# Background modulation of a two-layer diffusion backbone: a third of the dot products as GpSimd product and ScalarE sum, or all of them on VectorE

## The chip, the core and the metric

The kernel runs on one core of a Trainium2 chip. The metric is device time in microseconds for one launch; a change is judged by the median of several runs of the kernel before and of the kernel after. Engines are called by the names that the profile uses: PE (matmul), DVE (VectorE), ACT (ScalarE), POOL (GpSimd), SP (the queue that issues the loads).

## The reference, cut to what matters

The model has two layers. Each is a half-step feed-forward stage, a token mixer and a second feed-forward stage, and each of these takes shift, scale and gate vectors that come from the conditioning. These vectors are what this case is about:

```
for l in range(DEPTH):
    m_lat = (silu(c)     @ mod_w[l] + mod_b[l])   # 9 vectors of 1024 for the 512 latent tokens
    m_ctx = (silu(c_ctx) @ mod_w[l] + mod_b[l])   # the same weights, for the 256 context tokens
    h_lat = ffn_sublayer(h_lat, m_lat, 0, ...)    # rmsnorm, modulate, SwiGLU, gate
    h_ctx = ffn_sublayer(h_ctx, m_ctx, 0, ...)
    ...                                           # mixer, second feed-forward
```

`mod_w[l]` has 1024 x 9216 elements. The kernel holds it transposed as 72 tiles of 128 x 1024 for each layer, so that one entry of the result is the dot product of a tile's row with a vector of 1024. A context vector is not needed for the last four ninths of layer 1.

## The kernel before, in words

**Feed-forward.** Weights come as units of 128 x 1024 float32 (`raw`, by `w_fetch`). Each is split into a high part on ACT (`whi`, L760) and a low part on DVE (`wlo`, L770), and each product runs as three matmuls (L869 to L871). The inner width of 2816 is cut into chunks of 6, 5, 5 and 6 rows. A row is a gate unit and an up unit, each of 8 x 3 matmuls of 512 columns and as many of 256, 96 matmuls for the row in all. Its end is the eviction: ACT takes silu of the gate (L1064), DVE multiplies by the up bank (L1067), ACT rounds to `gh` (L918) and DVE subtracts to `gl` (L921). When the rows of a chunk are done, `w2` multiplies them with the second weight matrix, one output row m after the other; the first m goes through the earlier rows of the chunk first and comes last to the last row, whose `gh` and `gl` it needs then. From the second chunk on, DVE adds its result to `y` (L1108).

**Background.** Of the 144 modulation tiles, 16 are worked in the start (`start`, not touched here), and 128 in the background of the first feed-forward stage by `mods_task`, sixteen tasks of 8 tiles. A task is a generator: `pump` gives it credit, 0.65 for each us of matmul time that the program has written out, and each `yield` takes some back. So background work is written into the engines' queues at points fixed by the program's order and not by the clock of the chip; each engine then goes through its own queue in order. A background dot product (`mod_dot`, L651) therefore stands in DVE's queue among the `wlo`, the evictions and the adds.

A tile of weights (`mw`) has three slots. `mw_get` takes the next one that is loaded; `mw_put` puts the tile on a list, and after the delay that it names `mw_free` closes the tiles up to it and has SP load as many new ones (`mw_load`, L626). SP also issues the loads of `raw` (L749), in order.

Before the change, a tile with t divisible by 3 has its last dot product (the context's, or the latent one where there is no context) worked in two steps: POOL multiplies the tile in place by the vector (L667), and ACT copies it in place with a running sum (L668), written when the tile is freed. The 96 tiles with a context hold 32 such products, the 32 tiles without one hold 10.

At the end of a task, DVE adds the bias to the results (L680).

Of the kernel before, what the change touches and what calls it, by code (L numbers as in the profile page):

```python
# [12 lines left out]
AF = mybir.ActivationFunctionType  # L13
ALU = mybir.AluOpType
# [11 lines left out]
LAT, CTX = 0, 1  # L26
# [42 lines left out]
class Graph:  # L69
# [4 lines left out]
    LAT = 0.15  # L74
# [337 lines left out]
class Model:  # L412
# [241 lines left out]
    def mods_task(self, l, i, groups=(LAT, CTX)):  # L654

        nc = self.nc

        def gen():
            for t in range(i * 8, i * 8 + 8):
                w = self.mw_get()  # L660
                v = groups[-1]
                pool = t % 3 == 0
                if v == CTX or not pool:
                    self.mod_dot(w, l, t, LAT)
                    yield 1.14
                if pool:
                    nc.gpsimd.tensor_tensor(w, w, self.cb[v], op=ALU.mult)  # L667
                    self.mw_put(4.5, lambda w=w, t=t, v=v: nc.scalar.activation(w, w, AF.Copy,  # L668
                                                                                accum_out=self.modc[l][:, v, t:t + 1]))
                else:  # L670
                    if v == CTX:
                        self.mod_dot(w, l, t, v)
                    self.mw_put(1.5, lambda: None)
                yield 0.6
            yield 3.0
            self.mw_free(3)
            s = slice(i * 8, i * 8 + 8)
            bias = self.vec(f"mod_b{l}")[:, s]
            for v in groups:
                nc.vector.tensor_tensor(self.modc[l][:, v, s], self.modc[l][:, v, s], bias, op=ALU.add)  # L680
            self.bg_done.add((l, i))
            yield 0.2
        return ((l, i), gen())
# [2207 lines left out]
```

## Time and profile before

| | |
|---|---|
| median of 3 runs | 3002.24 us (2994.0 to 3002.37) |
| profiled execution, its own time | 3001.87 us |
| its span, first to last instruction | 2999.9 us |
| mean granted clock of PE | 0.966 |

The profile counts an engine as busy while an instruction of the program is on it, a stretched one too. Of the granted clock 1.00 is 2.4 GHz and 0.50 is 1.2 GHz. A row of a timeline gives start and duration in us, and in brackets the idle time ahead of it with what ended that. Matmul records overlap, since they are pipelined, so the distance between starts says more than the duration. A group's line ends with busy time and mean ns of one, then the idle time ahead of the group and what ended most of it.

### The profile page before, as it was taken

The page shows a single profiled execution, that of the slowest core. Times are in us where ns is not written, and L with a number is a line of the kernel's source. Part 1 is how long each engine was busy: PE and PEld are TensorE (multiplying, and loading weights), DVE is VectorE, ACT ScalarE, POOL GpSimd, SP SyncE. Part 2 cuts the span into 40 slices and gives each one's busy share as a digit, 9 for nine tenths or more (in the row PEclk, how much of TensorE's full clock was granted, in tenths as well). Part 3 has the DMA queues.
Part 4 walks back from the last instruction along what each step waited for, and adds up shares of the span by engine and source line. Part 5 has one row for each costly group of instructions (what it writes and reads, how often), then busy time and mean ns, then how long its engine had stood idle before and what let it go on. Part 6 is the DMA issues. An engine that isn't in the chain of part 4 may idle for free. (4 is left out here: it accounts for less than half of the span.)

```text
span 2999.9 us, 42053 instructions
## 1 busy us (share of the span) xinstructions
PE 2838.6 (95%) x16008; PEld 2456.4 (82%) x16008; DVE 1852.1 (62%) x3201; ACT 1084.4 (36%) x1897; POOL 898.4 (30%) x1281
## 2 busy tenths in 40 slices
PE   4999899989999989999999899999998899999997
PEld 3888778877778778888888788888887897888886
DVE  8799989675588667544544753543637694543334
ACT  3433223344477653222213432212224443432222
POOL 4122222352355350243344543343345000300001
PEclk7999999999799999999999899999999999999998
DMA  6365656633000223323233332232333563233332
GB/s 247 105 212 183 203 180 215 239 104 131 6 24 22 82 88 97 100 75 98 71 102 100 96 113 88 79 95 81 91 94 104 183 204 105 92 106 97 97 103 70
DMA packets 140808, 343.55 MB, mean 115 GB/s; under 512 B 13632, under 2 KB 61248, under 8 KB 138560
## 3 DMA queue, kind: packets, MB, share of 16 engines
q1 hardware_dynamic: 140608, 340.88, 35.2%
q8 instruction: 126, 2.06, 0.3%
q14 instruction: 74, 0.61, 0.1%
HBM read 311.53 MB, written 29.29 MB: 114 GB/s over the span
## 5 line engine op out<-in xcount | busy, mean ns | idle before, releaser
L869 PE MATMUL mm<-ahi,whi 128*128 128x512 f32 (+1 forms) x2128 | 740.0, 348 | 20.9 <-ACT ahi L555 16.7
L870 PE MATMUL mm<-alo,whi 128*128 128x512 f32 (+1 forms) x2128 | 735.7, 346 | 10.7 <-DVE alo L556 7.1
L871 PE MATMUL mm<-ahi,wlo 128*128 128x512 f32 (+1 forms) x2128 | 728.5, 342 | 4.6 <-DVE wlo L770 4.6
L770 DVE TENSOR_TENSOR wlo<-raw,whi 128x1024 fp32r<-128x1024 f32 (+2 forms) x391 | 461.4, 1182 | 376.0 <-ACT whi L760 360.4
L760 ACT ACTIVATE whi<-raw 128x1024 fp32r<-128x1024 f32 (+2 forms) x411 | 392.8, 956 | 296.8 <-PE mm L870 161.7
L869 PEld LDWEIGHTS mm<-ahi,whi 128*128 128x128 f32 x2128 | 406.7, 191 | 80.2 <-ACT ahi L555 18.8
L870 PEld LDWEIGHTS mm<-alo,whi 128*128 128x128 f32 x2128 | 406.7, 191 | 61.9 <-DVE alo L556 9.7
L871 PEld LDWEIGHTS mm<-ahi,wlo 128*128 128x128 f32 x2128 | 405.5, 191 | 55.6 <-DVE wlo L770 5.5
L869 PE MATMUL mm<-gh,whi 128*128 128x512 f32 x992 | 350.8, 354 | 13.5 <-ACT gh L918 13.5
L870 PE MATMUL mm<-gl,whi 128*128 128x512 f32 x992 | 349.8, 353 | 1.2 <-DVE gl L921 1.2
L871 PE MATMUL mm<-gh,wlo 128*128 128x512 f32 x992 | 346.8, 350 | 1.4 <-DVE wlo L770 1.4
L651 DVE SCALAR_TENSOR_TENSOR mj<-mw,cb 128x1024 bf16<-128x1024 f32 x182 | 262.6, 1443 | 24.5 <-DMA mw<-in_mod_wT_dram 21.8
L918 ACT ACTIVATE gh<-tmp 128x512 fp32r<-128x512 f32 (+1 forms) x135 | 73.7, 546 | 491.8 <-DVE tmp L1067 490.7
L667 POOL TENSOR_TENSOR mw<-mw,cb 128x1024 f32<-128x1024 f32 x42 | 116.3, 2770 | 379.2 <-DVE mj L651 320.9
L869 PEld LDWEIGHTS mm<-gh,whi 128*128 128x128 f32 x992 | 188.4, 190 | 43.3 <-ACT gh L918 14.9
L2171 POOL TENSOR_TENSOR s5t<-s5pw,s5bb 128x256 f32<-128x256 f32 x128 | 87.0, 708 | 440.4 <-PE mm L2182 353.5
L871 PEld LDWEIGHTS mm<-gh,wlo 128*128 128x128 f32 x992 | 187.8, 189 | 27.9 <-DVE wlo L770 1.9
L870 PEld LDWEIGHTS mm<-gl,whi 128*128 128x128 f32 x992 | 188.3, 190 | 27.1 <-DVE gl L921 2.8
L907 POOL TENSOR_TENSOR S<-S,tmp 128x512 f32<-128x512 f32 (+1 forms) x25 | 27.3, 1094 | 596.7 <-ACT tmp L906 596.2
L1067 DVE TENSOR_TENSOR tmp<-tmp,mm 128x512 f32<-128x512 f32 (+1 forms) x135 | 77.5, 574 | 186.3 <-PE mm L871 186.3
L279 POOL TENSOR_TENSOR S<-S,tmp 128x256 f32<-128x256 f32 (+3 forms) x116 | 134.5, 1162 | 135.4 <-ACT tmp L276 128.7
L1064 ACT ACTIVATE tmp<-mm 128x512 f32<-128x512 f32 (+1 forms) x135 | 63.0, 506 | 274.1 <-PE mm L871 274.1
(463 smaller groups left out, 5188.8 us busy)
## 6 DMA issues: line engine op xcount, KB each, us to landing
raw<-in_w_dram SPq DMA_DIRECT2D x210, 512.0 KB, 3.7
mw<-in_mod_wT_dram SPq DMA_DIRECT2D x128, 512.0 KB, 4.3
raw<-in_w_dram SPq DMA_DIRECT2D x88, 384.0 KB, 3.1
raw<-in_w_dram SPq DMA_DIRECT2D x64, 320.0 KB, 3.0
raw<-in_w_in_dram SPq DMA_DIRECT2D x23, 512.0 KB, 3.5
m0d<-in_mod_wT_dram SPq DMA_DIRECT2D x16, 512.0 KB, 8.0
raw<-in_w_out_dram SPq DMA_DIRECT2D x16, 512.0 KB, 3.3
s5v<-s5v SPq DMA_DIRECT2D x64, 128.0 KB, 3.0
```

Source lines behind the costliest of these rows:

```text
L279: add = lambda e: lambda: e.tensor_tensor(S(), S(), q["t"][:, :n], op=ALU.add)
L651: self.nc.vector.scalar_tensor_tensor(junk, w, 1.0, self.cb[v], op0=ALU.mult, op1=ALU.mult, accum_out=self.modc[l][:, v, t:t + 1])
L667: nc.gpsimd.tensor_tensor(w, w, self.cb[v], op=ALU.mult)
L760: self.nc.scalar.activation(hi[:, :n], raw[:, :n], AF.Copy)
L770: (eng or self.nc.vector).tensor_tensor(lo[:, :n], raw[:, :n], hi[:, :n].bitcast(F32), op=ALU.subtract)
L869: mm(out, whi, xhi, start=first, stop=False)
L870: mm(out, whi, xlo, start=False, stop=False)
L871: mm(out, wlo, xhi, start=False, stop=last)
L918: nc.scalar.activation(hi, src, AF.Copy)
L1064: nc.scalar.activation(st["s", jj, q][:, :n], bk[g][:, cs], AF.Silu)
L1067: nc.vector.tensor_tensor(t[:, :n], t[:, :n], bk[g][:, cs], op=ALU.mult)
L2171: g_.tensor_tensor(o, x, y, op=ALU.mult)
```

## The change

`mods_task` no longer tells tiles apart. For each group (latent, and context where there is one) it runs `mod_dot` on DVE. The product on POOL and the sum on ACT are gone from this task. Every tile is put on the list to be freed with a delay of 1.5 (before: 4.5 where POOL had the product). The credit of a tile with both groups stays 1.14 and 0.6. For a tile with the latent group alone it is 1.14; before, it was 1.14 and 0.6, or 0.6 alone where POOL had it.

```
-                v = groups[-1]
-                pool = t % 3 == 0
-                if v == CTX or not pool:
-                    self.mod_dot(w, l, t, LAT)
-                    yield 1.14
-                if pool:
-                    nc.gpsimd.tensor_tensor(w, w, self.cb[v], op=ALU.mult)
-                    self.mw_put(4.5, lambda w=w, t=t, v=v: nc.scalar.activation(w, w, AF.Copy,
-                                                                                accum_out=self.modc[l][:, v, t:t + 1]))
-                else:
-                    if v == CTX:
-                        self.mod_dot(w, l, t, v)
-                    self.mw_put(1.5, lambda: None)
-                yield 0.6
+                for v in groups:
+                    self.mod_dot(w, l, t, v)
+                    if v != groups[-1]:
+                        yield 1.14
+                self.mw_put(1.5, lambda: None)
+                yield 0.6 if len(groups) > 1 else 1.14
```

## Rows read from the trace of the kernel before

**Rows 1.** The page, busy time of each engine, its share of the span and its instructions.

```profile
PE 2838.6 (95%) x16008; PEld 2456.4 (82%) x16008; DVE 1852.1 (62%) x3201; ACT 1084.4 (36%) x1897; POOL 898.4 (30%) x1281
```

**Rows 2.** The waits of PE from 137 to 600 us: who waited for what, us in total, times, longest.

```profile
PE mm L869 <- ACT gh L918: 13.5, 3, 7.0
PE mm L871 <- DVE wlo L770: 1.4, 1, 1.4
```

**Rows 3.** The timeline of PE, at the first rows of a chunk's first unit (218.03) and around the ends of three chunks: the first matmul on `gh` after each chunk's last row, and the first that needs that last row.

```profile
218.03 0.40 PE L869 MATMUL mm<-ahi,whi 128*128 128x512 f32 x1
...
302.02 0.40 PE L869 MATMUL mm<-gh,whi 128*128 128x512 f32 x1
...
313.42 0.80 PE L869 MATMUL mm<-gh,whi 128*128 128x512 f32 x1 [7.04 <-ACT gh L918]
...
438.98 0.40 PE L869 MATMUL mm<-gh,whi 128*128 128x512 f32 x1
...
451.31 0.79 PE L869 MATMUL mm<-gh,whi 128*128 128x512 f32 x1 [6.27 <-ACT gh L918]
...
580.67 0.39 PE L869 MATMUL mm<-gh,whi 128*128 128x512 f32 x1
...
584.45 0.51 PE L869 MATMUL mm<-gh,whi 128*128 128x512 f32 x1 [0.22 <-ACT gh L918]
```

**Rows 4.** Windows behind the two long waits of PE: stretch and its length, then busy us and instructions of PE, PEld, DVE, ACT and POOL, then the granted clock, the share of the DMA engines and GB/s.

```profile
313.40:319.70 6.30, 5.31 (x14) 3.96 (x15) 5.57 (x11) 2.71 (x5) 1.19 (x1) 0.50 0.33 109
319.70:325.00 5.30, 5.30 (x31) 4.58 (x31) 4.40 (x8) 0.74 (x1) 0.00 (x0) 1.00 0.77 264
...
451.30:456.20 4.90, 4.89 (x13) 3.64 (x14) 4.38 (x8) 2.71 (x5) 0.00 (x0) 0.50 0.42 140
```

**Rows 5.** The timeline of DVE: the evictions L1067 of rows of a chunk, two dot products one behind the other, an undisturbed `gl`, the add that PE released, and the dot product ahead of the eviction at 449.92.

```profile
239.02 0.68 DVE L1067 TENSOR_TENSOR tmp<-tmp,mm 128x512 f32<-128x512 f32 x1
...
294.71 0.69 DVE L921 TENSOR_TENSOR gl<-tmp,gh 128x512 fp32r<-128x512 f32 x1 [0.70 <-ACT gh L918]
...
296.56 1.22 DVE L651 SCALAR_TENSOR_TENSOR mj<-mw,cb 128x1024 bf16<-128x1024 f32 x1
...
297.82 1.22 DVE L651 SCALAR_TENSOR_TENSOR mj<-mw,cb 128x1024 bf16<-128x1024 f32 x1
...
312.03 0.68 DVE L1067 TENSOR_TENSOR tmp<-tmp,mm 128x512 f32<-128x512 f32 x1
...
323.68 1.02 DVE L1108 TENSOR_TENSOR y<-mm,y 128x512 f32<-128x512 f32 x2 [0.90 <-PE mm L871]
...
446.75 3.24 DVE L651 SCALAR_TENSOR_TENSOR mj<-mw,cb 128x1024 bf16<-128x1024 f32 x1
...
449.92 0.68 DVE L1067 TENSOR_TENSOR tmp<-tmp,mm 128x512 f32<-128x512 f32 x1
```

**Rows 6.** The timeline of POOL from 445 to 448 us.

```profile
445.59 3.32 POOL L667 TENSOR_TENSOR mw<-mw,cb 128x1024 f32<-128x1024 f32 x1 [9.52 <-DVE mj L651]
```

**Rows 7.** The instructions of one line of the code, duration in ns as least, median and most, with the first and last start: the dot product (whole run), `wlo` (140 to 590 us), the bias add (137 to 600 us), the product on POOL and the sum on ACT.

```profile
L651 DVE SCALAR_TENSOR_TENSOR mj<-mw,cb x182: 1208/1224/3433, 138.1 to 593.9; 128x1024 bf16<-128x1024 f32 x182
...
L770 DVE TENSOR_TENSOR wlo<-raw,whi x61: 812/1216/3419, 140.5 to 586.2; 128x1024 fp32r<-128x1024 f32 x34, 128x640 fp32r<-128x640 f32 x16, 128x768 fp32r<-128x768 f32 x11
...
L680 DVE TENSOR_TENSOR modc<-modc,vecs x27: 150/160/2372, 165.9 to 574.5; 128x8 f32<-128x8 f32 x27
...
L667 POOL TENSOR_TENSOR mw<-mw,cb x42: 2347/2408/3444, 145.5 to 587.1; 128x1024 f32<-128x1024 f32 x42
...
L668 ACT ACTIVATE mw<-mw x42: 1039/1060/1066, 148.0 to 593.9; 128x1024 f32<-128x1024 f32 x42
```

**Rows 8.** Groups of DVE by line and shape, 170 to 239 us (the second chunk up to the eviction at 239.02; POOL starts six products in it).

```profile
L651 DVE SCALAR_TENSOR_TENSOR mj<-mw,cb 128x1024 bf16<-128x1024 f32 x32 | 45.7, 1430 | 2.7 <-DMA mw<-in_mod_wT_dram 2.1
...
L770 DVE TENSOR_TENSOR wlo<-raw,whi 128x1024 fp32r<-128x1024 f32 x4 | 7.1, 1770 | 0.0
L680 DVE TENSOR_TENSOR modc<-modc,vecs 128x8 f32<-128x8 f32 x4 | 2.8, 712 | 1.9 <-ACT mw L668 1.9
```

**Rows 9.** The same view, 239 to 312 us (up to the eviction at 312.03; POOL starts six products in it).

```profile
L651 DVE SCALAR_TENSOR_TENSOR mj<-mw,cb 128x1024 bf16<-128x1024 f32 x33 | 48.1, 1456 | 2.8 <-DMA mw<-in_mod_wT_dram 2.3
...
L921 DVE TENSOR_TENSOR gl<-tmp,gh 128x512 fp32r<-128x512 f32 x4 | 5.3, 1324 | 2.8 <-ACT gh L918 2.8
```

**Rows 10.** The same view, 323.6 to 449.9 us (from the add that PE released to the eviction at 449.92; POOL starts eleven products in it).

```profile
L651 DVE SCALAR_TENSOR_TENSOR mj<-mw,cb 128x1024 bf16<-128x1024 f32 x54 | 79.0, 1463 | 3.2 <-DMA mw<-in_mod_wT_dram 2.3
L770 DVE TENSOR_TENSOR wlo<-raw,whi 128x1024 fp32r<-128x1024 f32 x10 | 14.4, 1440 | 1.6 <-ACT whi L760 1.6
L921 DVE TENSOR_TENSOR gl<-tmp,gh 128x512 fp32r<-128x512 f32 x4 | 4.9, 1236 | 2.8 <-ACT gh L918 2.8
...
L680 DVE TENSOR_TENSOR modc<-modc,vecs 128x8 f32<-128x8 f32 x8 | 3.2, 437 | 1.2 <-ACT mw L668 1.2
```

**Rows 11.** The waits of DVE from 137 to 600 us.

```profile
DVE mj L651 <- DMA mw<-in_mod_wT_dram: 21.8, 23, 3.6
```

**Rows 12.** Groups of DVE by line and shape, 505 to 600 us, where the tiles have no context group.

```profile
L651 DVE SCALAR_TENSOR_TENSOR mj<-mw,cb 128x1024 bf16<-128x1024 f32 x22 | 32.6, 1481 | 14.9 <-DMA mw<-in_mod_wT_dram 14.9
```

**Rows 13.** DMA issues from 505 to 600 us: the loads of `mw` tiles, their number, size and median us from issue to landing.

```profile
mw<-in_mod_wT_dram SPq DMA_DIRECT2D x30, 512.0 KB, 4.6
```

**Rows 14.** A window over the last chunk's rows, columns as in Rows 4.

```profile
492.00:581.00 89.00, 89.00 (x482) 76.87 (x481) 66.23 (x86) 31.91 (x51) 28.58 (x11) 1.00 0.71 246
```

## The prediction, as it was put on record

> **What bounds the kernel now.** I read the page first: PE is busy for 95% of the span [rows 1], so an edit to work on other engines can only give or take PE's waits, and the clock that is lost behind them. The background runs from the first dot product at 138 us to the last at 594 us [rows 7], so I read PE's waits in that stretch: 13.5 us for `gh` and 1.4 us for `wlo` [rows 2]. The timeline of PE places them [rows 3]: 7.04 us up to 313.42 and 6.27 us up to 451.31, both in the first `w2` unit after a chunk's rows, at the matmul that needs the chunk's last row. The third chunk end, at 580.67, has two hiccups, the first of 0.22 us [rows 3].
>
> Behind each of the two waits the granted clock is 0.50 for a while. From 313.4 PE issues 14 matmuls in 6.3 us, where it issues 31 in 5.3 us at 1.00 [rows 4]; 14 are worth 2.4 us, so 3.9 us are lost. From 451.3 it issues 13 in 4.9 us, worth 2.2 us, so 2.7 us are lost. The first chunk end therefore costs 7.0 + 3.9 = 10.9 us, the second 1.4 + 6.3 + 2.7 = 10.4 us. Together **21.3 us** is all that this stage has to give.
>
> Why is `gh` late? It waits for the eviction L1067 on DVE, and DVE is behind. PE leaves the last row of the chunk at 302.02 [rows 3] and DVE starts its eviction at 312.03 [rows 5]: a lag of 10.0 us, of which the first 3.0 cost nothing (10.0 less the wait of 7.0). At the second end the lag is 449.92 - 438.98 = 10.9 us, of which 10.9 - 7.7 = 3.2 are free; at the third it is about 2.4 us, with some 2 free. DVE's queue is thus the bound wherever its lag at a chunk end exceeds 3 us, and the change is to be costed as DVE time ahead of these three evictions.
>
> **The change part by part.**
>
> *Added on DVE:* 42 dot products, one for each product on POOL [rows 7]. One takes 297.82 - 296.56 = 1.26 us from start to start with its readout [rows 5], 53 us in all.
>
> *Removed from POOL:* 42 products of 2.41 us median [rows 7]. POOL itself holds nothing up, but DVE stands still beside it. The product of 445.59 lasts until 448.9 [rows 6]; the dot product that starts on DVE at 446.75 takes 3.24 us [rows 5] where the median is 1.22 [rows 7]: 2.0 us in which DVE does nothing, just ahead of the eviction at 449.92. I size this by groups against undisturbed durations (dot product 1.224, `wlo` 1.216, bias add 0.160 [rows 7], `gl` 0.69 [rows 5]). From 239 to 312 us: 33 x (1.456 - 1.224) = 7.7 for the dots and 4 x (1.324 - 0.69) = 2.5 for `gl` [rows 9], 10.2 us for six products. From 323.6 to 449.9: 54 x 0.239 = 12.9, 10 x 0.224 = 2.2, 4 x 0.546 = 2.2 and 8 x 0.277 = 2.2 [rows 10], 19.5 us for eleven products. A product thus costs DVE 1.7 to 1.8 us, and the dot that replaces it costs 1.26: DVE comes out ahead by half a us each time. The rows give the range for one product, from nothing (where DVE has nothing to do) to 2.2 us (3.43 less 1.22 [rows 7]).
>
> The Trainium skill has a rule for this, in "SBUF — State Buffer", section "Who interferes with whom": VectorE instructions with two SBUF inputs and GpSimd instructions that read SBUF take one shared read interface as an exclusive lock for a whole instruction. The rows agree on the direction: `gl` and the dots, with two SBUF inputs, are stretched, and the eviction L1067 at 449.92, which reads a PSUM bank, takes 0.68 us as elsewhere. Taken at its word, each product would hold a busy DVE for its full 2.4 us, 26 us for the eleven where the rows show 19.5, and the second chunk end would lose its whole wait; the time would be about 2981.
>
> *Removed from ACT:* 42 sums of 1.06 us [rows 7] with their readouts. ACT is not the bound, but the bias add waits for the last sum of some tasks: 1.9 us [rows 8] and 1.2 us [rows 10], which DVE gets back.
>
> *The freeing of tiles:* a POOL tile used to be freed after product and sum; now it is free after DVE's second dot. SP issues its load earlier, and behind it in SP's queue stand the loads of `raw`. They cannot suffer from this, since the load now waits for less. DVE waits 21.8 us in all for `mw` tiles [rows 11], 2.3 us in each of the two stretches above; I take half of these 2.3 as gone, with none and all as bounds.
>
> *The first chunk end.* At 239.02 the lag is 4.2 us: five rows fill 218.03 to 302.02, so the first ends at 234.8 [rows 3, 5]. From 170 to 239 DVE loses to POOL at least 32 x 0.206 + 4 x 0.554 + 4 x 0.552 = 11.0 us and to ACT's sum 1.9 [rows 8], and would pay 6 x 1.26 = 7.6 for the new dots: 5.3 us better, so the lag goes to zero there, and cannot go below. From there the old lag grows by 10.0 - 4.2 = 5.8. The new one grows by 5.8 - 10.2 + 7.6 = 3.2, less 0 to 2.3 for the loads, plus 0 to 1.3, as the trace doesn't show whether the seventh dot comes ahead of the eviction: 0.9 to 4.5, and I take 2.7. Free are 3.0. The wait is gone, or up to 1.5 us.
>
> *The second chunk end.* In the old run PE's wait lets DVE catch up: at 323.68 PE releases DVE [rows 5], a lag of zero. In the new run it doesn't, and I carry 2.6 us on. The old lag grows from there by 10.9; the new one by 10.9 - 19.5 + 11 x 1.26 - 1.2 = 4.1, less 0 to 2.3. With the carry 4.4 to 6.7, of which 3.2 are free: a wait of 1.2 to 3.5 us, and I take 2.3. The old waits that brought the clock down were two to three times as long, so I charge no clock; if it falls, 2.7 us more [rows 4].
>
> *The last tiles, without context.* Ten products go and ten dots come, 12.6 us. By credit the 32 tiles took 22 x 1.74 + 10 x 0.6 = 44.3 and take 32 x 1.14 = 36.5, so the background ends 7.8 / 0.65 = 12 us of matmul time earlier and is denser: one dot in 1.14 / 0.65 = 1.75 us. Here DVE is not full, 66.2 of 89 us [rows 14], but waits for tiles, 14.9 us [rows 12]. I charge 0 to 2 us at the third chunk end, and take 1.
>
> *Sum:* 21.3 - 0 - 2.3 - 1.0 = 18.0 us. Of the profiled execution's 3001.87 us (span 2999.9 and 2.0 around it) that leaves 2983.9; the median of the runs is 0.4 us higher. I predict **2984 us**, with 2980 to 2990 as this case's own range.
>
> **The rivals.**
>
> *Only the first wait goes.* The second chunk end loses its catch-up of 10.9 us; if the relief between 323.6 and 449.9 falls where DVE would have waited anyway, the wait stays above 3 us and the clock falls again: 7.7 + 2.7 stay, and 2991 results. For it: the `whi` and tile waits of 1.6 and 3.2 us in that stretch [rows 10]. Against: the evictions there are late throughout.
>
> *No change.* DVE's lag is set by the supply of tiles and not by its own work: what POOL no longer takes becomes waiting for loads, and both waits stay: 3002. Against: 2.3 us of such waits in each stretch beside 10 and 19.5 us of stretching.
>
> *Slower: dots starve at the last chunk.* A slot is loaded again only after its dot, the delay of 1.5, and 4.6 us from issue to landing [rows 13]: 1.26 + 1.5 + 4.6 = 7.4 us for three tiles, 2.5 us for each where credit asks for one in 1.75. A waiting dot blocks the evictions behind it. If each of the 32 dots waits w, DVE needs 32w + 12.6, less 22 x 0.257 = 5.7 of stretching that goes [rows 12], and has 89 - 66.2 = 22.8 us idle [rows 14]. What is over, less 2 us that are free, delays PE at the third chunk end, with 3 us of clock. The mean wait now is 14.9 / 22 = 0.7 us [rows 12]. Above w = 1.1 us this eats the 19 us that the first two ends give. At twice the present mean, 1.4 us, the stall is 45 + 12.6 - 5.7 - 22.8 - 2 + 3 = 30, and the time 3002 - 19 + 30 = 3013. Against: the loads of the denser tiles are asked for earlier too, and each task ends with a pause of 3.0 in credit.
>
> *The change doesn't do what it says:* the code leaves no such case. One is left out of the sum: that an unseen cause, and not POOL, stretches DVE. Then 53 us come on top of a full queue; I give it 1 in 50 and count it with slower.
>
> **How the numbers follow.** Forecast 0.60, first wait only 0.14, no change 0.15, slower 0.11. Runs of this kernel can tell about 0.3% (9 us) from no change. The first two cases are faster by more (18 and 11 us), the third is the same, the last slower: 0.74, 0.15, 0.11. The low end is the full 21.3 us and 3 us for the spread of medians, 2977. The high end takes in the second case and the part of the third that gains 5 us, 2997.
>
> **What would show it.** After: no product on POOL before 600 us, 224 background dots, none above 1.3 us; `gl` of 512 at 0.7; no wait of PE near 302 to 313, and one under 4 us at the second chunk end; DVE's lag there 4 to 7 us; last dot earlier by some 25 to 30 us. The prediction is wrong if dots stay stretched, if DVE's waits for tiles grow by more than 15 us, or if PE's wait at the third chunk end passes 3 us.

## The result, and the profile after

The changed kernel took **2974.52 us** (median of 4 runs, 2971.21 to 2978.33) against 3002.3 before (4 runs, 2994.0 to 3002.42): a ratio of 0.9919, with a 95% interval from 0.9900 to 0.9937. It is faster by about 0.8%. The forecast was 2984 and its range ended at 2977, so the median lies 2.5 us beyond the low end. The same kernel run again later gave 2979.19, inside the range (below). By count, 42 of 224 background dot products change their engine: the third in the title is a third of the tiles, each of which has its last dot moved.

The profiled execution took 2978.33 us, 23.5 us less than that of before. The line numbers behind `mods_task` are 8 lower in it: L861 to L863 are the three matmuls, L762 is `wlo`, L913 `gl`, L1059 the eviction. The waits of PE from 137 to 600 us, against [rows 2]:

```profile
PE mm L861 <- ACT gh L910: 0.8, 1, 0.8
PE mm L862 <- DVE gl L913: 0.2, 1, 0.2
```

Of 13.5 us of waits for `gh` 0.8 is left. The background dots, against the first line of [rows 7]:

```profile
L651 DVE SCALAR_TENSOR_TENSOR mj<-mw,cb x224: 1209/1224/1228, 138.7 to 563.2; 128x1024 bf16<-128x1024 f32 x112
```

None of the 224 is above 1.228 us, where the longest of 182 took 3.433. The timeline of PE at the three chunk ends, against [rows 3]:

```profile
302.70 0.40 PE L861 MATMUL mm<-gh,whi 128*128 128x512 f32 x1
...
307.89 0.50 PE L861 MATMUL mm<-gh,whi 128*128 128x512 f32 x1 [0.83 <-ACT gh L910]
...
432.50 0.40 PE L861 MATMUL mm<-gh,whi 128*128 128x512 f32 x1
...
563.48 0.39 PE L861 MATMUL mm<-gh,whi 128*128 128x512 f32 x1
```

PE leaves the last of these rows at 563.48 and not at 580.67: 17.2 us are gained by then. The timeline of DVE, against [rows 5]: three evictions of the second chunk, the add that PE released, and the evictions at the two later chunk ends.

```profile
235.70 0.69 DVE L1059 TENSOR_TENSOR tmp<-tmp,mm 128x512 f32<-128x512 f32 x1 [1.43 <-PE mm L863]
...
252.50 0.69 DVE L1059 TENSOR_TENSOR tmp<-tmp,mm 128x512 f32<-128x512 f32 x1 [1.28 <-PE mm L863]
...
306.49 0.68 DVE L1059 TENSOR_TENSOR tmp<-tmp,mm 128x512 f32<-128x512 f32 x1
...
317.20 1.02 DVE L1100 TENSOR_TENSOR y<-mm,y 128x512 f32<-128x512 f32 x2 [1.00 <-PE mm L863]
...
433.10 0.68 DVE L1059 TENSOR_TENSOR tmp<-tmp,mm 128x512 f32<-128x512 f32 x1
...
565.24 0.68 DVE L1059 TENSOR_TENSOR tmp<-tmp,mm 128x512 f32<-128x512 f32 x1
```

The lags are 306.49 - 302.70 = 3.8 us at the first chunk end (10.0 before), 0.6 at the second (10.9) and 1.8 at the third (2.4). At 235.70 and 252.50 DVE itself waits for PE. The groups of DVE from 317 to 433.2 us, against [rows 10]:

```profile
L651 DVE SCALAR_TENSOR_TENSOR mj<-mw,cb 128x1024 bf16<-128x1024 f32 x65 | 79.4, 1222 | 1.4
L762 DVE TENSOR_TENSOR wlo<-raw,whi 128x1024 fp32r<-128x1024 f32 x10 | 12.2, 1220 | 0.5 <-ACT whi L752 0.5
...
L913 DVE TENSOR_TENSOR gl<-tmp,gh 128x512 fp32r<-128x512 f32 x4 | 2.8, 693 | 2.8 <-ACT gh L910 2.8
...
L672 DVE TENSOR_TENSOR modc<-modc,vecs 128x8 f32<-128x8 f32 x8 | 0.9, 158 | 0.0
```

65 dots take DVE 79.4 us where 54 took 79.0 [rows 10], and nothing is stretched. The idle time is smaller too: no wait for an `mw` tile (2.3 us before), none for a sum (1.2), and 0.5 for `whi` (1.6).

I measure the first two chunk ends by PE's `w2` phase, from its first matmul on `gh` to its first on the next chunk. The two windows, columns as in [rows 4]:

```profile
302.70:348.50 45.80, 44.62 (x242) 38.09 (x241) 43.03 (x77) 7.50 (x10) 0.00 (x0) 0.96 0.61 204
432.50:474.50 42.00, 42.00 (x242) 36.77 (x241) 40.54 (x72) 7.51 (x10) 0.00 (x0) 1.00 0.65 218
```

A phase without a wait takes 42.00 us. The first end still costs 3.8 us, the second nothing. Behind the wait of 0.8 us at the first end the granted clock was 0.50 for a while:

```profile
310.00:313.40 3.40, 3.40 (x11) 2.92 (x12) 3.36 (x8) 0.74 (x1) 0.00 (x0) 0.50 0.35 101
```

### The profile page after: what moved, and what is told of

Same layout as the page of the kernel before. It is cut to its first block, busy times and chain, and to the rows that moved or that the text cites. A ratio compares the mean times of both kernels' runs of the same rounds, so it can differ in the third digit from the quotient of the medians.

```text
span 2976.5 us, 42015 instructions
## 1 busy us (share of the span) xinstructions
PE 2825.5 (95%) x16008; PEld 2445.7 (82%) x16008; DVE 1837.2 (62%) x3285; ACT 1039.1 (35%) x1813; POOL 777.4 (26%) x1239
## 5 line engine op out<-in xcount | busy, mean ns | idle before, releaser
L861 PE MATMUL mm<-ahi,whi 128*128 128x512 f32 (+1 forms) x2128 | 740.6, 348 | 21.2 <-ACT ahi L555 16.7
L863 PE MATMUL mm<-ahi,wlo 128*128 128x512 f32 (+1 forms) x2128 | 728.7, 342 | 4.6 <-DVE wlo L762 4.6
L762 DVE TENSOR_TENSOR wlo<-raw,whi 128x1024 fp32r<-128x1024 f32 (+2 forms) x391 | 452.5, 1159 | 380.9 <-ACT whi L752 363.0
L861 PEld LDWEIGHTS mm<-ahi,whi 128*128 128x128 f32 x2128 | 407.0, 191 | 80.7 <-ACT ahi L555 18.8
L863 PEld LDWEIGHTS mm<-ahi,wlo 128*128 128x128 f32 x2128 | 405.5, 191 | 55.5 <-DVE wlo L762 5.5
L861 PE MATMUL mm<-gh,whi 128*128 128x512 f32 x992 | 349.3, 352 | 0.9 <-ACT gh L910 0.8
L863 PE MATMUL mm<-gh,wlo 128*128 128x512 f32 x992 | 345.9, 349 | 0.0
L651 DVE SCALAR_TENSOR_TENSOR mj<-mw,cb 128x1024 bf16<-128x1024 f32 x224 | 273.7, 1222 | 16.2 <-DMA mw<-in_mod_wT_dram 11.9
L861 PEld LDWEIGHTS mm<-gh,whi 128*128 128x128 f32 x992 | 187.7, 189 | 30.0 <-issue 1.8
L863 PEld LDWEIGHTS mm<-gh,wlo 128*128 128x128 f32 x992 | 187.0, 188 | 26.1
L1059 DVE TENSOR_TENSOR tmp<-tmp,mm 128x512 f32<-128x512 f32 (+1 forms) x135 | 77.6, 575 | 188.6 <-PE mm L863 188.6
L1100 DVE TENSOR_TENSOR y<-mm,y 128x512 f32<-128x512 f32 (+1 forms) x128 | 71.1, 586 | 111.2 <-PE mm L863 111.1
```

The source lines that it names most:

```text
L651: self.nc.vector.scalar_tensor_tensor(junk, w, 1.0, self.cb[v], op0=ALU.mult, op1=ALU.mult, accum_out=self.modc[l][:, v, t:t + 1])
L762: (eng or self.nc.vector).tensor_tensor(lo[:, :n], raw[:, :n], hi[:, :n].bitcast(F32), op=ALU.subtract)
L861: mm(out, whi, xhi, start=first, stop=False)
L863: mm(out, wlo, xhi, start=False, stop=last)
L1059: nc.vector.tensor_tensor(t[:, :n], t[:, :n], bk[g][:, cs], op=ALU.mult)
L1100: nc.vector.tensor_tensor(y, bk[g][:, :n_], y, op=ALU.add)
```

## The experiments

Two theories stood against each other, with a third for the sums. **A:** the product on POOL stops DVE, DVE's lag at the chunk ends makes PE wait. **B:** the denser and earlier end of the tiles without context gains. **C:** the sums on ACT, and the late freeing of tiles through them, held DVE up.

### The kernel before, again

Nothing edited.

> The kernel before once more, with nothing altered, for a second profile of it. The background stage repeats: waits of 6 to 8 us for gh at the first and second chunk end. Of the 23 us between the first two profiles, 5.5 arose between 690 and 1110 us, where the change alters nothing. If that was the first profile's chance, this one is 3 to 10 us shorter in that stretch; if it belongs to the change, it repeats within 2 us. Median 2994 to 3004.

Median 2999.74 us (10 runs, 2994.07 to 3005.65). The two `w2` phases:

```profile
302.41:355.53 53.12, 44.92 (x243) 38.44 (x242) 49.63 (x75) 12.92 (x20) 13.45 (x5) 0.90 0.56 193
439.53:492.39 52.86, 46.39 (x243) 39.44 (x241) 50.88 (x78) 13.54 (x23) 11.66 (x4) 0.90 0.61 201
```

The stage repeats: 53.12 + 52.86 - 2 x 42.0 = 22.0 us are lost in the two phases, 3.8 in the changed kernel, a gain of 18.2 us. PE waits 7.2 us for `gh` at the first end, and at the second 4.7 for `gh` and 1.8 for `wlo`, where 6 to 8 for `gh` were expected. The later stretch did not come out shorter; it is taken up in the last section.

### Only the tiles with a context, only those without

```
+                if len(groups) > 1:
+                    for v in groups:
...
+                else:
+                    v = groups[-1]
+                    pool = t % 3 == 0
...
```

The second kernel has `== 1` in the first line.

> Only the 96 tiles with a context group follow the change (32 products of POOL become dots on DVE); the 32 tiles without one keep product, sum and the old credit. Theory A (a product on POOL stops DVE for about 1.7 us, and DVE's lag at the chunk ends is what PE waits for): the waits of 7.0 and 6.3 us before 480 us are gone as in the changed kernel, at most 1 us of PE's waits for gh is left, and the time is that of the changed kernel within 4 us, 2971 to 2980. Theory B (the denser, earlier end of the last tiles is what gains): the time is near the old one, 2996 to 3003.

> The other half: only the 32 tiles without a context group follow the change, the 96 others keep product and sum. Theory A: both waits of PE stay as they were, 7 and 6 us, and the time stays within 4 us of the old one, 2994 to 3004. Theory B: 2970 to 2985.

The context part alone took 2972.24 us (5 runs; ratio 0.9924, 0.9898 to 0.9950), the other part alone 3001.33 us (10 runs; 0.9999, 0.9983 to 1.0014). The `w2` phases of the context part:

```profile
302.38:346.63 44.25, 43.05 (x243) 36.79 (x241) 42.48 (x77) 7.50 (x10) 0.00 (x0) 1.00 0.63 212
430.63:472.63 42.00, 42.00 (x243) 36.75 (x241) 40.54 (x72) 7.51 (x10) 0.00 (x0) 1.00 0.65 216
```

and of the other part:

```profile
303.31:354.33 51.02, 44.48 (x242) 38.06 (x241) 48.38 (x73) 12.81 (x20) 11.86 (x5) 0.93 0.58 196
438.33:490.90 52.57, 44.63 (x242) 37.90 (x241) 50.48 (x78) 13.53 (x23) 11.46 (x4) 0.94 0.62 202
```

B falls: as far as the intervals tell, the whole gain comes from the 32 products of tiles with a context. The other part loses 51.02 + 52.57 - 84.0 = 19.6 us in the two phases, 2.4 less than the kernel before (again), though the tiles that it alters come only behind them [rows 12]: such sums can differ by 2 us from one profile to the next. The context part also shows what the clock adds. It has the same 0.8 us wait at the first end as the changed kernel, but its clock stays at 1.00 and its phase is 1.5 us shorter.

### An idle product, and an idle memset

The dots of the changed kernel, and work for POOL that nobody reads:

```
+                if t % 3 == 0:
+                    nc.gpsimd.tensor_tensor(w, w, self.cb[groups[-1]], op=ALU.mult)
-                self.mw_put(1.5, lambda: None)
+                self.mw_put(4.5 if t % 3 == 0 else 1.5, lambda: None)
```

In the second kernel the multiplication is `nc.gpsimd.memset(w, 0.0)`.

> The changed kernel, and after the last dot of every third tile POOL multiplies the tile in place by the vector; nobody reads that product, and no sum follows on ACT. The results are those of the changed kernel. Theory A: the dots and the gl are stretched again (most of the 42 products by 1.5 to 2.2 us of DVE), on top of the dots that DVE now has: the lag at the first two chunk ends is 15 to 25 us, PE waits 12 to 22 us at each, and the time is 3015 to 3040. Theory C (it was the sum on ACT and the late freeing through it that held DVE up): no such waits, 2972 to 2985.

> As the idle-product kernel, but POOL fills the tile with zeros by a memset after the last dot, in place of the multiplication: it writes as much and reads nothing. Nothing is left out. Theory A1 (DVE stops because POOL's product reads its operands): the dots and the gl are not stretched (dots at 1.22, none above 1.3), and the time is that of the changed kernel, 2968 to 2983. Theory A2 (any instruction of POOL on these tiles stops DVE, or holding the slot longer does): stretched dots or waits for tiles, and 3000 to 3043.

With the product 3043.17 us (4 runs; ratio 1.0152, 1.0128 to 1.0176), with the memset 2973.35 us (4 runs; 0.9909, 0.9885 to 0.9933). The groups of DVE with the idle product, 137 to 640 us:

```profile
L651 DVE SCALAR_TENSOR_TENSOR mj<-mw,cb 128x1024 bf16<-128x1024 f32 x224 | 306.7, 1369 | 17.1 <-DMA mw<-in_mod_wT_dram 12.5
L764 DVE TENSOR_TENSOR wlo<-raw,whi 128x1024 fp32r<-128x1024 f32 x35 | 67.8, 1938 | 3.5 <-ACT whi L754 3.5
L915 DVE TENSOR_TENSOR gl<-tmp,gh 128x512 fp32r<-128x512 f32 x18 | 18.9, 1048 | 12.6 <-ACT gh L912 12.6
```

The dots are at 1.37 us on average, the `wlo` at 1.94 and the `gl` at 1.05, with no sum on ACT at all: the stretching comes from POOL's product. PE's waits up to 650 us there:

```profile
PE mm L865 <- DVE wlo L764: 24.2, 10, 4.5
PE mm L863 <- ACT gh L912: 20.1, 4, 8.8
```

The time is 3 us above what A allowed, and the place was not quite foreseen: DVE is so late that PE waits 24.2 us for `wlo`, most of it within the rows, before a chunk end is reached. At the first two chunk ends it then waits 8.8 and 4.9 us for `gh`, where A put 12 to 22 at each. The memset on POOL and the dots beside it:

```profile
L666 POOL MEMSET mw<- x42: 952/956/961, 147.3 to 560.2; 128x1024 f32 x42
```

```profile
L651 DVE SCALAR_TENSOR_TENSOR mj<-mw,cb x224: 1214/1224/1227, 138.7 to 562.4; 128x1024 bf16<-128x1024 f32 x112
```

No dot of 224 is above 1.227 us beside 42 memsets of 0.96 us; by the two timelines 35 dots overlap a memset. So holding the tile longer stretches no dot here, and writing it stretches none either. The Trainium skill says the latter in "SBUF — State Buffer", section "Who interferes with whom": a VectorE instruction with two SBUF inputs contends with a GpSimd one that reads SBUF and not with one that only writes it; these two runs agree.

### Without the sums

```
-                    self.mw_put(4.5, lambda w=w, t=t, v=v: nc.scalar.activation(w, w, AF.Copy, accum_out=...))
+                    self.mw_put(4.5, lambda: None)
```

Here and in the next kernel the results are set to zero at the start.

> The kernel before with its 42 products on POOL, but without the sums on ACT: 42 of the dot products stay at zero, and a tile is free as soon as POOL is done with it. Theory A: the products still stop DVE, both waits of PE stay at 5 us or more each; DVE gets back only the 6.7 us that the bias adds waited for a sum, a part of it ahead of a chunk end: 2988 to 3003. Theory C (the sums and what they delay): the waits go, 2968 to 2983.

Median 2996.35 us (10 runs; ratio 0.9991, 0.9977 to 1.0006). The `w2` phases, and the eviction at the first chunk end:

```profile
302.68:347.30 44.62, 43.06 (x242) 36.83 (x241) 42.99 (x69) 7.52 (x10) 10.05 (x4) 1.00 0.63 207
431.30:480.30 49.00, 44.18 (x242) 37.95 (x241) 47.57 (x71) 7.51 (x10) 11.44 (x4) 0.97 0.63 200
...
305.78 0.68 DVE L1068 TENSOR_TENSOR tmp<-tmp,mm 128x512 f32<-128x512 f32 x1
```

The time is where A put it, but A is wrong on the first chunk end: with every product still on POOL, its cost falls to 2.6 us and its lag to 305.78 - 302.68 = 3.1. PE waits 1.3 us there and 4.8 at the second end, where A put 5 or more at each. C has its share. The groups of DVE from 236 to 305.8 us, against [rows 9]:

```profile
L653 DVE SCALAR_TENSOR_TENSOR mj<-mw,cb 128x1024 bf16<-128x1024 f32 x32 | 43.4, 1356 | 0.7
L771 DVE TENSOR_TENSOR wlo<-raw,whi 128x1024 fp32r<-128x1024 f32 x6 | 9.5, 1589 | 0.0
L922 DVE TENSOR_TENSOR gl<-tmp,gh 128x512 fp32r<-128x512 f32 x4 | 5.3, 1327 | 2.8 <-ACT gh L919 2.8
```

The stretching is there, 32 x 0.132 + 6 x 0.373 + 4 x 0.637 = 9.0 us. What is gone is the waiting for `mw` tiles (2.3 us in [rows 9], none here) and, ahead of this stretch, 1.9 us for a sum [rows 8]; the stretch now begins with no lag (DVE waits for PE ahead of its eviction at 235.68), where the kernel before had 4.2 us. The second end still costs 7.0 us. And a new wait appears at the third, in PE's timeline:

```profile
580.60 0.79 PE L870 MATMUL mm<-gh,whi 128*128 128x512 f32 x1 [6.00 <-ACT gh L919]
```

Of the 3.4 us by which the median is below that of the kernel before run beside it nothing is proven, as the interval holds 1.

### Neither products nor dots

```
-                    nc.gpsimd.tensor_tensor(w, w, self.cb[v], op=ALU.mult)
-                    self.mw_put(4.5, lambda w=w, t=t, v=v: nc.scalar.activation(...))
+                    self.mw_put(1.5, lambda: None)
```

> The kernel before without its 42 products and sums, and with no dots in their place: 42 of the dot products are left out (their results stay at zero), the tiles are loaded all the same. Theory A: DVE has 53 us less than in the changed kernel, and all that can still be gained is the 3.8 us that the changed kernel loses at the first chunk end: 2968 to 2976, with no wait of PE for gh. If 53 us of dots cost more than these 4 us, then the added dots do press on DVE somewhere that I don't see: below 2965.

Median 2972.39 us (4 runs; ratio 0.9911, 0.9887 to 0.9935), with both phases at 42.00 us:

```profile
303.58:345.58 42.00, 42.00 (x243) 36.75 (x241) 36.49 (x65) 7.51 (x10) 0.00 (x0) 1.00 0.64 214
```

In these two phases the 53 us of dots that the change adds cost no more than the 3.8 us of the first end. The median can't resolve even these.

### A slower pace, after and before

```
-        self.rate = 0.65
+        self.rate = 0.62
```

> The changed kernel with the background's rate at 0.62 in place of 0.65. If DVE's lag at the first chunk end is the sum of what stands ahead of the eviction, the background is written some 5% later and the lag there falls from 3.8 to 1 to 3 us: no wait for gh and no fall of the clock there, 2 to 4 us less than the changed kernel in PE's work between 300 and 350 us. The last dot comes about 20 us later, at 580 to 590 us, and still ahead of the end of the stage; the median is then 2967 to 2980. If the lag at the chunk end is set by where the dots happen to stand, it stays between 3 and 5 us and nothing is gained.

> The kernel before, products and sums kept, with the background's rate at 0.62 in place of 0.65. If the lag at a chunk end is the sum of DVE's work and waits ahead of the eviction, some 5% fewer dots stand there (two dots' time in the first stretch, three in the second): lag 5 to 8 us at the first end and 7 to 10 at the second, waits of 2 to 5 and 4 to 7 us, PE's work in the two w2 phases together 5 to 12 us shorter, median 2986 to 2998. If pace is no lever, both waits stay above 6 us.

On the changed kernel 2974.86 us (4 runs; ratio 0.9918, 0.9893 to 0.9942), on the one before 3002.5 us (10 runs; 1.0014, 0.9999 to 1.0030). The phases of the first of the two, then of the second:

```profile
302.78:345.08 42.30, 42.27 (x243) 36.75 (x242) 40.81 (x72) 7.52 (x10) 0.00 (x0) 1.00 0.66 211
429.08:471.23 42.15, 42.15 (x243) 36.75 (x241) 40.69 (x73) 7.51 (x10) 0.00 (x0) 1.00 0.65 215
```

```profile
302.36:348.34 45.98, 44.38 (x242) 37.98 (x241) 42.27 (x67) 11.65 (x18) 11.08 (x4) 0.96 0.59 204
432.34:485.25 52.91, 44.35 (x243) 38.00 (x241) 49.28 (x78) 12.70 (x21) 11.01 (x4) 0.90 0.62 206
```

On the changed kernel the phases fall by another 3.4 us and the lag at the first end to 304.62 - 302.78 = 1.8, as expected; the last dot starts at 578.3, a little ahead of the 580 to 590 put. The median doesn't show the gain, so it is no proven improvement.

On the kernel before, the expectation failed. The first end's cost falls to 4.0 us and the second's stays at 10.9. The lags are 305.85 - 302.36 = 3.5 and 443.87 - 432.34 = 11.5 us, where 5 to 8 and 7 to 10 were expected, and the median is above the 2986 to 2998 put. This is what the rival "only the first wait goes" forecast, but not its mechanism, the lost catch-up. DVE still catches up behind the first end, at an add that PE released, and the lag grows from zero as in the kernel before. That add, and the dots from there to 443.8:

```profile
322.29 1.02 DVE L1108 TENSOR_TENSOR y<-mm,y 128x512 f32<-128x512 f32 x2 [0.41 <-PE mm L871]
...
L651 DVE SCALAR_TENSOR_TENSOR mj<-mw,cb 128x1024 bf16<-128x1024 f32 x51 | 78.3, 1536 | 7.0 <-DMA mw<-in_mod_wT_dram 6.2
```

The 51 dots take DVE 78.3 us, where 54 took 79.0 in a stretch 5 us longer, and wait 6.2 us for `mw` tiles instead of 2.3 [rows 10]. Why the tiles come later there was not looked into. That kernel's last dot comes at 687.8 us, in the next stage, and the median gains nothing.

### The changed kernel, again

> The changed kernel once more, with nothing altered, to see how its median and its stages repeat: the background stage must give the same within 1 us (one wait for gh below 1 us, the first chunk end), while the stages between 690 and 1110 us of PE's span, which the change doesn't touch, differ from profile to profile by several us with the granted clock. Median 2968 to 2981.

Median 2979.19 us (4 runs, 2977.02 to 2982.13; ratio 0.9927, 0.9912 to 0.9942). The phases are 45.79 and 42.00 us, the first with the same wait of 0.8. The stage repeats within 0.01 us; the median moved by 4.7.

## Why the prediction came out as it did

The sign held, and the mechanism (DVE's lag at the chunk ends, stretched by POOL's products) held at the second chunk end; at the first the waits behind the sums did more. The stage gave 17.2 us by PE's timeline and 18.2 by its two phases, where the sum said 18.0. That the sum fits so well is luck: it charged 3.8 us too little at the first end and 2.3 + 1.0 too much at the other two.

*Added dots and the stretching.* 224 dots at 1.222 us, none stretched, as put; the last starts 30.7 us earlier, where 25 to 30 was put. That POOL's product causes the stretching is shown by the idle product, which brings it back with no sum behind it. That it is the product's reading fits the memset, which stretches nothing; but the memset is also shorter, and no instruction that reads in another way was run. The prediction read the eviction at 449.92 as one that a product leaves alone; it starts after that product's end at 448.9 and shows nothing. The line of all evictions of the kernel before does:

```profile
L1067 DVE TENSOR_TENSOR tmp<-tmp,mm x36: 407/546/690, 130.2 to 583.0; 128x256 f32<-128x256 f32 x18, 128x512 f32<-128x512 f32 x18
```

By the timelines eleven of them overlap a product, and none takes above 0.69 us. The rule that a product holds a busy DVE for its full time gives too much: the eleven ahead of the second end cost 19.5 us and not 26. The products are stretched as well, from 2.35 up to 3.44 us [rows 7], so a part of the loss is POOL's.

*The first chunk end.* Forecast lag 0.9 to 4.5, taken 2.7; measured 3.8. The wait of 0.8 us lies within the 0 to 1.5 put, though the signs named none near 302 to 313. Its cost was mis-sized: taken 0, measured 3.8. PE is idle for 45.80 - 44.62 = 1.2 us, the clock takes 1.5 (against the context part alone; the 11 matmuls in 3.4 us at 0.50 are worth 1.9 at 1.00 by [rows 4], which says the same), and the rest is matmuls further apart. At the second end the prediction charged no clock because the old waits, behind which it fell, were two to three times as long as the one forecast. Here it fell behind 0.8 us, and in the context part it stayed at 1.00 behind the same wait: the length of the wait alone does not tell.

The cause was misread too. I credited this end with 10.2 us of stretching against 7.6 of new dots, and with half of the 2.3 us of waits for tiles. In the run without sums the stretching stays, 9.0 us, and the lag falls to 3.1 all the same; the changed kernel, with dots for products, has 3.8. So at this end taking away the sums, and with them the holding of tiles, is enough for the gain, and with the sums gone the trade of product for dot is worth about nothing. What the trade alone would give with the sums kept was not run.

*The second chunk end.* Forecast lag 4.4 to 6.7 and a wait of 2.3; measured 0.6 and none. The wait went wholly, as the rule of the full time would have had it, but not by that price. Two terms failed. The carry of 2.6 us is not there: PE's first output row at the first end took 7.6 us (302.70 to 310.32), where an eighth of an undisturbed phase is 5.25, and behind it DVE is 0.4 us late; at 317.20 PE releases it. The first two lines are the changed kernel, the others the context part, where the clock stayed at 1.00:

```profile
310.32 0.63 PE L861 MATMUL mm<-gh,whi 128*128 128x512 f32 x1
310.75 1.01 DVE L1100 TENSOR_TENSOR y<-mm,y 128x512 f32<-128x512 f32 x2
...
309.88 0.40 PE L877 MATMUL mm<-gh,whi 128*128 128x512 f32 x1
310.43 1.02 DVE L1116 TENSOR_TENSOR y<-mm,y 128x512 f32<-128x512 f32 x2
...
431.75 0.68 DVE L1075 TENSOR_TENSOR tmp<-tmp,mm 128x512 f32<-128x512 f32 x1
```

There too the carry is about 0.5 us, the lag at the second end is 431.75 - 430.63 = 1.1, and that end costs nothing. So the slower clock gave at most the last half us. And the waits for tiles went wholly, with 1.1 us for `whi` besides, so that the 4.1 us of growth become 4.1 - 2.3 - 1.1 = 0.7. Here the stretching matters: without the sums alone the lag is still 7.6 us.

*The last tiles.* Taken 1.0, measured nothing: lag 1.8, no wait of PE in the list. DVE's waits for `mw` tiles from 137 to 600 us fell from 21.8 [rows 11] to 11.9:

```profile
DVE mj L651 <- DMA mw<-in_mod_wT_dram: 11.9, 14, 2.1
```

So the rival "slower" had the wrong sign, which fits that a dot on DVE frees its slot sooner than product and sum did.

*The whole.* 18.0 us were forecast. Between the two first profiled executions lie 23.5: 17.2 arise in the stage and 6.8 in the stretch of the last section, less 0.5 elsewhere. Between the first medians lie 27.8, and 20.6 between the changed kernel's second median and the 2999.78 us of the kernel before run beside it. The sum had no term for anything outside the stage, and its low end allowed 21.3 us and 3 of spread; that is the step by which the first median came out below it. Where the medians differ beyond the stage no profile shows.

## What to carry to other kernels

Work on POOL is not always off DVE: here a product cost DVE 1.7 to 1.8 us beside it and spared it a dot of 1.26. Before work is moved to POOL to spare DVE, look in the trace for DVE instructions that grow beside it, and charge POOL's work to DVE's queue. Cost a queue by its lag at the points where another engine needs it, and count waits and stretching there as well as work; here one wait went with the sums alone, and the next only with the products. Look for the point behind a wait at which the late engine has caught up before a lag is carried on to the next one.

## What the runs showed that I had not expected

The stretch after the stage, from the attention's first normalisations to the end of the first layer, has the same work in all kernels here, and differs by up to 13 us. Its window in the kernel before (again), in the changed kernel, in the changed kernel (again), with only the tiles without context changed, and in the kernel before at the slower pace:

```profile
730.90:1164.40 433.50, 409.55 (x2341) 348.61 (x2340) 297.01 (x549) 264.82 (x577) 174.81 (x156) 0.93 0.17 55
```

```profile
713.20:1140.70 427.50, 402.84 (x2341) 343.40 (x2340) 296.78 (x549) 264.43 (x577) 173.57 (x156) 0.95 0.17 56
```

```profile
711.60:1141.70 430.10, 405.29 (x2345) 345.60 (x2344) 296.84 (x550) 264.35 (x577) 174.58 (x156) 0.94 0.17 56
```

```profile
731.90:1152.80 420.90, 395.31 (x2341) 335.87 (x2341) 296.50 (x549) 264.29 (x577) 173.55 (x156) 0.97 0.17 57
```

```profile
739.90:1161.60 421.70, 396.10 (x2344) 336.13 (x2343) 296.54 (x549) 264.47 (x577) 174.11 (x156) 0.97 0.18 57
```

The instructions and DVE's busy time agree; PE's granted clock goes from 0.93 to 0.97 as the stretch goes from 433.5 to 420.9 us. The first profile of the kernel before took 434.3 here, 6.8 more than the changed kernel's first. By the expectation for the second profile, a repeat within 2 us meant that this belongs to the change. The last two windows speak against that: both kernels keep products and sums in the tiles with a context, and both are shorter here than the changed kernel. What sets the clock here stays open, and so does whether the changed kernel gets a higher one more often. The runs of the unchanged kernel lie between 2988 and 3006 us, the shortest with a mean clock of 0.977 over the run and the longest with 0.969; that this stretch makes their difference is likely but not shown, since these runs were not profiled.

The clock also decides what a short wait costs: the wait of 0.8 us at the first chunk end came with a mean clock of 0.96 over the phase in both profiles of the changed kernel, and with 1.00 in the context part alone and beside the idle memset, whose phases (44.25 and 44.27 us) are 1.5 us shorter.
